# RWKV heads by column halves, and every engine's order from the library's timeline machine, in a two-layer hybrid decoder trunk

## The chip, the cores and the metric

One NeuronCore of a Trainium2 chip runs the whole program in one launch. The metric is the device time of that launch in microseconds (us), as the median of several runs. Engines are named as in the profile: PE (TensorE, the matmul engine, with its weight loads shown apart as PEld), DVE (VectorE), ACT (ScalarE), POOL (GpSimd), SP (SyncE, which issues DMAs).

## The reference

The input `x` is 1024 tokens by 1024 features, in float32. Each of two layers normalises it, projects it, runs four mixers side by side, gates and concatenates their outputs, projects back and adds a gated embedding:

```python
for i in range(DEPTH):
    proj = rms_norm(x, g_pre[i]) @ w_in[i]
    ...
    y_a = nsa_attention(...)
    y_b = spatial_gating(...)
    y_c = conv_module(...)
    y_d = rwkv7_time_mix(token_shift(rw, rwkv_mu[i]), ...)
    mix = jnp.concatenate([y_a * silu(z_a), y_b * silu(z_b), y_c * silu(z_c), y_d * silu(z_d)], axis=-1)
    x = x + rms_norm(mix @ w_out[i], g_post[i])
    x = x + sigmoid(x @ ple_gate[i]) * (p[i] @ ple_proj[i])
```

The change touches the fourth mixer, a recurrence over the tokens with one 64x64 state for each of four heads:

```python
def step(state, inp):
    r_t, w_t, k_t, v_t, kk_t, a_t = inp
    sa = einsum('bhvk,bhk->bhv', state, -kk_t)
    state = state * w_t + outer(sa, kk_t * a_t) + outer(v_t, k_t)
    return state, einsum('bhvk,bhk->bhv', state, r_t)
```

The attention mixer, whose matmuls share PE with it, has for every 128 queries and each of four heads three softmax branches: over compressed keys, over all earlier keys and over a window of 512.

## The kernel before

**Tiling.** Features lie on the 128 partitions and tokens along the free axis. The program goes through layer 0 and layer 1, each in two halves of 512 tokens. One letter of the strings `ORDER` (L32) stands for one stage of a half: `H` normalises, `F` prepares RWKV, `R` and `r` are its solve and its steps, `A` is one tile of 128 queries of attention, `a` to `d` and `N`, `G` are projections, `O`, `x`, `g` the output side. An `A` may belong to the half before. `run` emits the stages in this order, and `tail` (L1130) the end of the last half.

**Dense matmuls.** `mm3` (L161) forms one product of float32 precision from three matmuls of a high and a low part (L163, L164, L165). These are the dense matmuls below: mostly 128x512 each, the operands `aT` (activations) and `wh`, `wl` (weights, which `split_w`, L149, loads and splits), the results in PSUM banks named `mm`.

**PSUM.** Eight banks of 128x512: `mm` and `s` two each, `rp`, `pt`, `pv` and `c1` (shown as `c`) one each.

**Attention.** `branch` (L975) computes the scores into `s` (L994, L995), adds tables and takes maxima (L1014, L1018, L1022 on DVE), takes the exponential on ACT (L1024) and scales on DVE (L1029); its result is `r`. `attn_tile` then takes up to two blocks of keys for two heads at once: four transposes into the bank `pt` (L957), a copy to a high part on ACT (L960), a subtraction for the low part on DVE (L961), and two matmuls for each block into `pv` (L966, L967).

**RWKV.** A half has 8 chunks of 64 tokens. `rwkv_ab` (L509) forms for one chunk the matrices of the four heads (`a_block`, L430; L438 on PE into `rp` or `c1`; L516 on DVE masks them into `AT`, shown as `at`; L519, L521 transpose `BK` into `bkt`). `rwkv_solve` (L444) gets inverses of triangular 16 and 32 blocks of all heads and chunks with a loop on DVE: 15 rounds of L478 and L480, 16 of L500 and L502, through DRAM scratch `Nd` and `Xd`. `rwkv_tri` (L524) joins the blocks of a chunk to 64 (L533 on PE, L535 on DVE, L539 on PE, L541 on DVE, result `XF`). `rwkv_step` (L558) then moves the state `S` (two alternating tiles `SB`) over one chunk: four matmuls of one head each into `p1` (L578) and two of the state (L582), an ACT copy to `Wt` (L585, the tile `q`), four matmuls with `XF` (L589), copies into `uv` (the tile `l`) on DVE and ACT (L591, L592), four matmuls into `p3` (L602), four updates of the state on DVE (L611), four matmuls for the chunk's output (L616) and an ACT copy into `ytok` (L618, the tile `yt`). There are 32 steps: 8 for each of four halves.

In all of these matmuls of one head the four heads follow as 0, 1, 2, 3. Head `h` has pair `j = h // 2` and `e = h % 2`. L578, L533 and L616 write the same 64 output partitions for all four heads (L578 128 for head 0); L589 writes partitions 64 j to 64 j + 63; L602 those of e. Output partitions are the columns of PE's array, so L589 is in one column half for heads 0 and 1 and in the other for 2 and 3. The partitions of the operands are its row halves.

**What sets the order.** The kernel text gives a program order; the library's `TileContext` schedules every engine's instructions from it, with the program order as priority (weights are raised by `high_priority`, L151), and inserts the semaphore waits. Each engine then runs its list strictly in order: an instruction that waits holds up all behind it on the same engine. [...]

## Time and profile before

| | |
|---|---|
| median of 3 runs | 1925.44 us (1922.86 to 1941.99) |
| the profiled execution's own time | 1919.29 us |
| its span in the trace | 1917.6 us |
| mean granted PE clock in it | 0.954 |
| busy share: PE, DVE, ACT, POOL | 90%, 72%, 42%, 32% |

Shares are busy time over the span, of one execution. A row of a timeline gives start and duration in us, the engine, the line of the kernel, the operation, output and input tiles, their shapes, and how many equal instructions in a row it stands for. Matmuls overlap, and the end of one is modelled; the start of the next is the better measure of how long one took. DMA, at a third of its engines' time over the span, is not followed further here.

### The profile page before, as it was taken

The page shows a single profiled execution, that of the slowest core. Times are in us where ns is not written, and L with a number is a line of the kernel's source. Part 1 is how long each engine was busy: PE and PEld are TensorE (multiplying, and loading weights), DVE is VectorE, ACT ScalarE, POOL GpSimd, SP SyncE. Part 2 cuts the span into 40 slices and gives each one's busy share as a digit, 9 for nine tenths or more (in the row PEclk, how much of TensorE's full clock was granted, in tenths as well). Part 3 has the DMA queues.
Part 4 walks back from the last instruction along what each step waited for, and adds up shares of the span by engine and source line. Part 5 has one row for each costly group of instructions (what it writes and reads, how often), then busy time and mean ns, then how long its engine had stood idle before and what let it go on. Part 6 is the DMA issues. An engine that isn't in the chain of part 4 may idle for free. (4 is left out here: it accounts for less than half of the span.)

```text
span 1917.6 us, 27663 instructions
## 1 busy us (share of the span) xinstructions
PE 1725.0 (90%) x9444; PEld 1296.7 (68%) x9444; DVE 1383.7 (72%) x3361; ACT 813.6 (42%) x1805; POOL 612.2 (32%) x487
## 2 busy tenths in 40 slices
PE   5797998899799999899888999989988989989998
PEld 4565776566577667666666767766666767766777
DVE  4449787887888865977578881869778789476554
ACT  4332234544223455655232343545432445545543
POOL 2223343122342333322233346322232232422253
PEclk8898999999899999999998999999998999979999
DMA  6435233123432231532253233542253223223444
GB/s 208 90 87 107 71 97 84 45 57 64 114 81 78 67 99 63 169 106 55 60 123 78 69 115 117 166 121 56 62 113 79 53 57 115 66 72 109 139 139 152
DMA packets 326148, 182.23 MB, mean 95 GB/s; under 512 B 88300, under 2 KB 299248, under 8 KB 326008
## 3 DMA queue, kind: packets, MB, share of 16 engines
q1 hardware_dynamic: 326008, 180.47, 34.7%
q8 instruction: 74, 1.21, 0.3%
q14 instruction: 66, 0.54, 0.1%
HBM read 149.98 MB, written 30.44 MB: 94 GB/s over the span
## 5 line engine op out<-in xcount | busy, mean ns | idle before, releaser
L158 POOL TENSOR_TENSOR wl<-ws,wh 128x512 fp32r<-128x512 f32 (+2 forms) x388 | 521.6, 1346 | 1160.7 <-ACT wh L157 1021.0
L163 PE MATMUL mm<-aT,wh 128*128 128x512 f32 (+1 forms) x1304 | 538.2, 416 | 16.6 <-ACT t L667 7.4
L164 PE MATMUL mm<-aT,wh 128*128 128x512 f32 (+1 forms) x1304 | 536.3, 411 | 8.3 <-DVE aT L252 8.0
L165 PE MATMUL mm<-aT,wl 128*128 128x512 f32 (+1 forms) x1304 | 535.4, 411 | 0.4 <-POOL wl L158 0.4
L157 ACT CAST wh<-ws 128x512 fp32r<-128x512 f32 (+2 forms) x388 | 236.9, 611 | 454.3 <-PE mm L164 229.4
L163 PEld LDWEIGHTS mm<-aT,wh 128*128 128x128 f32 (+1 forms) x1304 | 251.0, 193 | 71.0 <-ACT t L667 7.9
L164 PEld LDWEIGHTS mm<-aT,wh 128*128 128x128 f32 (+1 forms) x1304 | 252.1, 193 | 60.5 <-DVE aT L252 15.2
L165 PEld LDWEIGHTS mm<-aT,wl 128*128 128x128 f32 (+1 forms) x1304 | 251.6, 193 | 48.2 <-issue 2.6
L683 DVE SCALAR_TENSOR_TENSOR cv<-cv,cw,cv 128x512 f32<-128x512 f32 x240 | 213.4, 905 | 3.2
L961 DVE TENSOR_TENSOR pt<-pt,pt 128x512 fp32r<-128x512 f32 (+1 forms) x152 | 93.7, 617 | 122.2 <-ACT pt L960 120.9
L1024 ACT ACTIVATE r<-s,sma 128x512 f32<-128x512 f32 (+3 forms) x192 | 106.2, 555 | 111.2 <-DVE sma L1022 76.3
L960 ACT CAST pt<-pt 128x512 fp32r<-128x512 f32 (+1 forms) x152 | 80.3, 528 | 112.7 <-PE pt L957 112.3
L957 PE MATMUL pt<-cst,r 128*128 128x128 f32 x528 | 98.4, 282 | 21.9 <-DVE r L1029 16.9
L957 PEld LDWEIGHTS pt<-cst,r 128*128 128x128 f32 x528 | 64.2, 143 | 50.8 <-DVE r L1029 26.3
L967 PE MATMUL pv<-pt,vs 128*128 128x256 f32 x264 | 79.0, 317 | 11.8 <-DVE pt L961 10.2
L966 PE MATMUL pv<-pt,vs 128*128 128x256 f32 x264 | 84.7, 321 | 2.4 <-ACT pt L960 2.1
L994 PE MATMUL s<-kv,qs 128*128 128x512 f32 (+2 forms) x192 | 75.6, 394 | 4.9 <-ACT r L1024 4.7
L1029 DVE TENSOR_SCALAR r<-r,sma 128x640 f32<-128x640 f32 (+7 forms) x128 | 76.1, 595 | 0.8
L967 PEld LDWEIGHTS pv<-pt,vs 128*128 128x128 f32 x264 | 50.6, 192 | 35.1 <-DVE pt L961 28.3
L966 PEld LDWEIGHTS pv<-pt,vs 128*128 128x128 f32 x264 | 50.6, 192 | 32.3 <-ACT pt L960 26.7
L995 PE MATMUL s<-kv,qs 128*128 128x512 f32 (+2 forms) x192 | 65.7, 345 | 0.0
L994 PEld LDWEIGHTS s<-kv,qs 128*128 128x128 f32 x192 | 37.1, 193 | 34.5 <-ACT r L1024 27.2
(333 smaller groups left out, 2904.1 us busy)
## 6 DMA issues: line engine op xcount, KB each, us to landing
ws<-in_w_in_dram SPq DMA_DIRECT2D x232, 256.0 KB, 2.9
ws<-in_ple_gate_dram SPq DMA_DIRECT2D x64, 256.0 KB, 2.8
ws<-in_w_out_dram SPq DMA_DIRECT2D x60, 256.0 KB, 2.8
ped<-ot SPq DMA_DIRECT2D x32, 256.0 KB, 3.4
ld<-in_nsa_w_dram SPq DMA_DIRECT2D x32, 256.0 KB, 3.5
ld<-ped SPq DMA_DIRECT2D x32, 256.0 KB, 3.5
mixd<-y SPq DMA_DIRECT2D x30, 256.0 KB, 2.0
ld<-mixd SPq DMA_DIRECT2D x30, 256.0 KB, 3.0
```

Source lines behind the costliest of these rows:

```text
L157: nc.scalar.copy(hi[:, :cols], st[:, :cols])
L158: nc.gpsimd.tensor_sub(lo[:, :cols], st[:, :cols], hi[:, :cols].bitcast(F32))
L163: nc.tensor.matmul(out, lh, rh, start=first, stop=False, skip_group_check=shared)
L164: nc.tensor.matmul(out, lh, rl, start=False, stop=False, skip_group_check=shared)
L165: nc.tensor.matmul(out, ll, rh, start=False, stop=last, skip_group_check=shared)
L683: nc.vector.scalar_tensor_tensor(ac, xg[j][:, k:k + TH], cw[:, j * 31 + k:j * 31 + k + 1], ac, op0=OP.mult, op1=OP.add)
L957: nc.tensor.transpose(pt[:, o:o + 128], P[e][:, (b + x - b0) * 128:(b + x - b0) * 128 + 128], self.ident)
L961: nc.vector.tensor_sub(Tl[:, :n], pt[:, :n], Th[:, :n].bitcast(F32))
L966: nc.tensor.matmul(acc, vs, Th[:, x * 256:x * 256 + 256], start=False, stop=False)
L967: nc.tensor.matmul(acc, vs, Tl[:, x * 256:x * 256 + 256], start=False, stop=last)
L994: nc.tensor.matmul(p[:, :n], w.QS[hd][:, qs], w.KH[br, hh][:, c0 * 128:c1 * 128], start=True, stop=False)
L1024: nc.scalar.activation(P[:, o:o + wd], p[:, c:c + wd], AF.Exp, bias=ng[:, 0:1], accum_out=den[:, x:x + 1])
```

## The change

There are two edits.

**Heads by column halves.** The heads are taken in the order 0, 2, 1, 3, and the operands are laid out so that pair `j` writes the output partitions 64 j to 64 j + 63. For pair 1 the two halves of `AR`, and with them those of `AT`, change places, and the mask `C_MA` is 64 columns wider, so that pair 1 reads it 64 columns on. `XF` and `Wt` become 128 partitions by 128 columns, each pair in its own half. One operation on all four heads therefore becomes one on each pair in several places: L535 and L541 on DVE become two each, the copy to `Wt` becomes one on ACT and one on DVE (2 x 128 columns in place of 256), the copy into `ytok` two on ACT, and the transfer of the first four chunks of a half to `Nd` two on SP. `a_block` becomes `a_blocks`, which takes two banks and alternates its matmuls between them.

**The order.** `TileContext` is called with `schedule_with_timeline_sim=True`: the lists of all engines are computed anew, with the library's model of when each instruction would run. The program order and its priorities are unchanged.

```diff
-    def a_block(self, q, c, e, full):
+    def a_blocks(self, q, c, full):
-        pA = self.ps("c1" if self.solving and self.nb % 2 else "rp")
+        pA = [self.ps("rp"), self.ps("c1" if self.solving else "s")]
         for j in range(2):
-            bk, ar = self.BK[j][q][es, c], self.AR[j][q][es, c]
+            for e in range(2):
+                es = slice(64 * e, 64 * e + 64)
+                bk, ar = self.BK[j][q][es, c], self.AR[j][q][es, c]
...
     def rwkv_solve(self):
             self.rwkv_ab(c)
-            nc.sync.dma_start(Nd[:, c * 256:c * 256 + 256].rearrange("p (h t) -> p h t", h=4),
-                              self.AT[c][0:64, :, :, 0:64].rearrange("p a b c -> p (a b) c"))
+            for j in range(2):
+                nc.sync.dma_start(Nd[:, c * 256 + j * 128:c * 256 + j * 128 + 128].rearrange("p (h t) -> p h t", h=2),
+                                  self.AT[c][0:64, j, :, 64 * j:64 * j + 64])
...
     def rwkv_tri(self, c):
-        for h in range(4):
-            nc.tensor.matmul(pT[0:64, hs[h]], N[h], XY[0:64, hs[h]], start=True, stop=True)
+        for h in (0, 2, 1, 3):
+            j, e = divmod(h, 2)
+            nc.tensor.matmul(pT[pair[j], hs[h]], self.AT[c][0:64, j, e, pair[j]], XY[0:64, hs[h]], start=True, stop=True)
-        nc.vector.tensor_mul(T1, pT[0:64, :256].rearrange("p (a b) -> p a b", a=4),
-                             self.c[0:64, C_ML:C_ML + 64].unsqueeze(1).to_broadcast([64, 4, 64]))
+        for j in range(2):
+            nc.vector.tensor_mul(T1[:, 2 * j:2 * j + 2], pT[pair[j], cols[j]].rearrange("p (a b) -> p a b", a=2),
+                                 self.c[pair[j], C_ML:C_ML + 64].unsqueeze(1).to_broadcast([64, 2, 64]))
-        for h in range(4):
-            nc.tensor.matmul(pX[64:128, hs[h]], T1[:, h], XY[64:128, hs[h]], start=True, stop=True)
-        XF = self.t([64, 4, 64], "xf", bufs=4)
-        nc.vector.tensor_add(fl(XF), XY[64:128], pX[64:128, :256])
+        for h in (0, 2, 1, 3):
+            nc.tensor.matmul(pX[pair[h // 2], hs[h]], T1[:, h], XY[64:128, hs[h]], start=True, stop=True)
+        XF = self.t([128, 2, 64], "xf", bufs=4)
+        for j in range(2):
+            nc.vector.tensor_add(XF[pair[j]].rearrange("p a b -> p (a b)"), XY[64:128, cols[j]], pX[pair[j], cols[j]])
...
     def rwkv_step(self, c):
-        for h in range(4):
+        for h in (0, 2, 1, 3):
             hs = slice(h * 64, h * 64 + 64)
-            m = 64 if h else 128
-            nc.tensor.matmul(p1[:m, hs], AT[64:128, h // 2, h % 2, :m], uv[64:128, hs], start=(h == 0), stop=False,
+            j, e = divmod(h, 2)
+            nc.tensor.matmul(p1[pair[j], hs], AT[64:128, j, e, pair[j]], uv[64:128, hs], start=(e == 0), stop=False,
                              skip_group_check=True)
...
-        Wt = self.t([128, 256], "q1", bufs=1)[:64]
-        nc.scalar.copy(Wt, p1[0:64])
-            nc.tensor.matmul(p2[es, h % 2 * 64:h % 2 * 64 + 64], XF[:, h], Wt[:, hs], start=False, stop=True,
+        Wt = self.t([128, 256], "q1", bufs=1)[:, :128]
+        nc.scalar.copy(Wt[0:64], p1[0:64, 0:128])
+        nc.vector.tensor_copy(Wt[64:128], p1[64:128, 128:256])
+            nc.tensor.matmul(p2[pair[j], e * 64:e * 64 + 64], XF[pair[j], e], Wt[pair[j], e * 64:e * 64 + 64],
...
-            nc.tensor.matmul(p1[64:128, hs], AT[:n, h // 2, h % 2, 64:128], uv[:n, hs], start=False, stop=True,
+            nc.tensor.matmul(p1[pair[1 - j], hs], AT[:, j, e, pair[1 - j]], uv[:, hs], start=False, stop=True,
-        nc.scalar.copy(ytok[64 * (c % 2):64 * (c % 2) + 64], p1[64:128])
+        for j in range(2):
+            nc.scalar.copy(ytok[pair[c % 2], j * 128:j * 128 + 128], p1[pair[1 - j], j * 128:j * 128 + 128])
...
-    with _tile.TileContext(nc) as tc:
+    with _tile.TileContext(nc, schedule_with_timeline_sim=True) as tc:
```

Lines of the functions behind `rwkv_solve` stand some numbers lower in the changed file: L578 is L582 there, L582 is L586, L589 is L593, L616 is L620, L957 is L962, L966 and L967 are L971 and L972.

Three places on PE show what the order does. The first is one RWKV step in the first half of layer 0. In before, PE's list has (`c_374` is the bank of the step, `mm` that of a projection, `x4` means four alike in a row):

```order
L578 MATMUL c_374_1685<-l_372_1678,at_1521 128x64
L578 MATMUL c_374_1685<-l_372_1678,at_1521 64x64 x3
L582 MATMUL c_374_1685<-SB_79,ab_447 128x128
L582 MATMUL c_374_1685<-SB_79,ab_629 128x128
L165 MATMUL mm_2337<-aT_306,wl_2359 128x512
L163 MATMUL mm_2337<-aT_311,wh_2358 128x512
L164 MATMUL mm_2337<-aT_312,wh_2358 128x512
L589 MATMUL c_374_1685<-q_375_1692,xf_1549 64x64 x4
L165 MATMUL mm_2337<-aT_311,wl_2359 128x512
L163 MATMUL mm_2337<-aT_316,wh_2358 128x512
```

The same step in the changed kernel:

```order
L582 MATMUL c_374_1717<-l_372_1710,at_1543 64x64 x4
L586 MATMUL c_374_1717<-SB_79,ab_447 128x128
L586 MATMUL c_374_1717<-SB_79,ab_629 128x128
L962 MATMUL pt_2909<-cst,r_638_2895 128x128
L962 MATMUL pt_2909<-cst,r_632_2881 128x128
L962 MATMUL pt_2909<-cst,r_638_2895 128x128
L593 MATMUL c_374_1717<-q_375_1724,xf_1572 64x64 x4
L999 MATMUL s_2973<-kv_1041,qs_1217 128x256
L1000 MATMUL s_2973<-kv_1042,qs_1217 128x256
L971 MATMUL pv_2879<-pt_2914,vs_1134 128x256
L606 MATMUL c_374_1717<-l_372_1710,bkt_1555 64x64 x4
```

Between the step's matmuls before has dense ones, and the changed kernel transposes, scores and products of attention, which an ACT and a DVE instruction must precede. The dense matmuls of this half have moved ahead of the steps: from one dense matmul of `mm_2551` to the next, of `mm_3792`, PE's list holds 379 others. I call this stretch A.

The second place is the loop of an attention tile late in the program. Before (one round of `pt_16374` and `pv_16317`, the dense matmuls of `mm_17531` among them):

```order
L957 MATMUL pt_16374<-cst,r_3924_16319 128x128
L957 MATMUL pt_16374<-cst,r_3931_16340 128x128
L957 MATMUL pt_16374<-cst,r_3924_16319 128x128
L957 MATMUL pt_16374<-cst,r_3931_16340 128x128
L163 MATMUL mm_17531<-aT_17154,wh_17552 128x512
L164 MATMUL mm_17531<-aT_17155,wh_17552 128x512
L165 MATMUL mm_17531<-aT_17154,wl_17553 128x512
L163 MATMUL mm_17531<-aT_17162,wh_17552 128x512
L966 MATMUL pv_16317<-pt_16379,vs_9393 128x256
L164 MATMUL mm_17531<-aT_17163,wh_17552 128x512
L165 MATMUL mm_17531<-aT_17162,wl_17553 128x512
L967 MATMUL pv_16317<-pt_16380,vs_9393 128x256
```

The same loop in the changed kernel, from its last dense matmul on:

```order
L165 MATMUL mm_18067<-aT_17831,wl_18089 128x512
L971 MATMUL pv_15643<-pt_15690,vs_9469 128x256
L972 MATMUL pv_15643<-pt_15691,vs_9469 128x256
L971 MATMUL pv_15643<-pt_15690,vs_9469 128x256
L972 MATMUL pv_15643<-pt_15691,vs_9469 128x256
L962 MATMUL pt_15698<-cst,r_3704_15645 128x128
L962 MATMUL pt_15698<-cst,r_3711_15665 128x128
L962 MATMUL pt_15698<-cst,r_3704_15645 128x128
L962 MATMUL pt_15698<-cst,r_3711_15665 128x128
L971 MATMUL pv_15643<-pt_15703,vs_9469 128x256
L972 MATMUL pv_15643<-pt_15704,vs_9469 128x256
L971 MATMUL pv_15643<-pt_15703,vs_9469 128x256
```

The transposes are now followed at once by the products that need them, with nothing between. This goes on for 277 matmuls, up to the `dense_short` of `tail` (stretch C). Between the two, in layer 1's first half, lies a third such stretch of 308 matmuls, in which PE transposes `bkt`, forms `at` and does attention while DVE has the whole loop of `rwkv_solve` (stretch B). It begins so:

```order
L165 MATMUL mm_9422<-aT_8691,wl_9444 128x512
L519 MATMUL rp_9140<-cst,ab_8823 128x128
L519 MATMUL rp_9140<-cst,ab_9005 128x128
L438 MATMUL c_2185_9165<-ab_8821,ab_8823 128x128
L438 MATMUL c_2185_9165<-ab_9003,ab_9005 128x128
L971 MATMUL pv_6586<-pt_6635,vs_1134 128x256
L972 MATMUL pv_6586<-pt_6636,vs_1134 128x256
```

In before the longest run of PE matmuls without a dense one is 68.

## Rows read from the trace of the kernel before

**Rows 1.** The page's first part: busy us (share of the span) x instructions.

```profile
PE 1725.0 (90%) x9444; PEld 1296.7 (68%) x9444; DVE 1383.7 (72%) x3361; ACT 813.6 (42%) x1805; POOL 612.2 (32%) x487
```

**Rows 2.** Windows: stretch, us; busy us of each engine (instructions); PE clock, DMA share, GB/s.

```profile
core 0: us, PE busy (x) PEld busy (x) DVE busy (x) ACT busy (x) POOL busy (x), PEclk, DMA share, GB/s
...
150.00:200.00 50.00, 36.63 (x201) 27.24 (x201) 45.18 (x81) 10.41 (x22) 13.75 (x11) 0.80 0.46 105
...
1000.00:1050.00 50.00, 43.12 (x222) 31.63 (x221) 45.18 (x65) 10.32 (x20) 15.49 (x12) 0.90 0.35 89
1150.00:1200.00 50.00, 48.09 (x211) 38.60 (x210) 7.32 (x21) 20.61 (x41) 30.41 (x24) 0.97 0.38 115
100.00:1900.00 1800.00, 1645.93 (x9124) 1239.60 (x9123) 1334.15 (x3252) 771.40 (x1734) 584.22 (x459) 0.96 0.34 93
```

**Rows 3.** Timeline of PE, 194 to 202: start us, duration us, instruction, [idle before].

```profile
196.27 0.63 PE L165 MATMUL mm<-aT,wl 128*128 128x512 f32 x1
...
200.54 0.45 PE L163 MATMUL mm<-aT,wh 128*128 128x512 f32 x1
```

**Rows 4.** Timeline of all engines, 1752 to 1755: a round of the attention loop.

```profile
1752.35 0.60 PE L957 MATMUL pt<-cst,r 128*128 128x128 f32 x4
...
1752.99 0.59 ACT L960 CAST pt<-pt 128x512 fp32r<-128x512 f32 x1 [2.45 <-PE pt L957]
1753.02 0.39 PE L165 MATMUL mm<-aT,wl 128*128 128x512 f32 x1
...
1753.25 0.40 PE L163 MATMUL mm<-aT,wh 128*128 128x512 f32 x1
...
1753.61 0.69 DVE L961 TENSOR_TENSOR pt<-pt,pt 128x512 fp32r<-128x512 f32 x1 [1.11 <-ACT pt L960]
...
1754.81 0.60 PE L957 MATMUL pt<-cst,r 128*128 128x128 f32 x4
```

**Rows 5.** Groups by form, PE: the first dense line; its two others are alike.

```profile
L163 PE MATMUL mm<-aT,wh 128*128 128x512 f32 x1272 | 525.6, 415 | 14.1 <-ACT t L667 7.4 <-DVE y L648 5.4 <-ACT ot L1103 0.4
```

**Rows 6.** Timeline of all engines, 294 to 301: one RWKV step.

```profile
294.28 0.92 PE L578 MATMUL c<-l,at 64*128 64x64 f32 x8 [0.46 <-ACT yt L618]
...
295.93 0.37 ACT L585 COPY q<-c 64x256 f32<-64x256 f32 x1 [1.71 <-PE c L582]
...
296.35 0.46 PE L589 MATMUL c<-q,xf 64*64 64x64 f32 x8 [0.28 <-ACT q L585]
...
297.25 0.26 ACT L592 COPY l<-c 64x128 f32<-64x128 f32 x1 [0.42 <-DVE l L591]
...
298.34 1.17 DVE L611 SCALAR_TENSOR_TENSOR SB<-c,gc,q 64x64 f32<-64x64 f32 x4
...
299.99 0.82 PE L616 MATMUL c<-l,at 64*64 64x64 f32 x8
```

**Rows 7.** Timeline of PE, 1527 to 1531: the matmuls of `rwkv_tri`.

```profile
1527.76 0.67 PE L533 MATMUL rp<-x,at 64*64 64x64 f32 x8
```

**Rows 8.** Groups of DVE: line, instruction xcount | busy us, mean ns | idle before.

```profile
L961 DVE TENSOR_TENSOR pt<-pt,pt 128x512 fp32r<-128x512 f32 (+1 forms) x152 | 93.7, 617 | 122.2 <-ACT pt L960 120.9 <-PE s L995 0.5
L1029 DVE TENSOR_SCALAR r<-r,sma 128x640 f32<-128x640 f32 (+7 forms) x128 | 76.1, 595 | 0.8
L1014 DVE CUSTOM_DVE_ANT_0 s<-s,T 128x256 f32<-128x256 f32 (+1 forms) x144 | 53.8, 374 | 2.4 <-PE s L995 1.7
...
L1018 DVE TENSOR_REDUCE sma<-s 128x1 f32<-128x256 f32 (+3 forms) x120 | 51.5, 432 | 0.5
L500 DVE TENSOR_TENSOR q<-l,q 128x128 f32<-128x128 f32 (+7 forms) x64 | 45.1, 705 | 2.1
L611 DVE SCALAR_TENSOR_TENSOR SB<-c,gc,q 64x64 f32<-64x64 f32 x112 | 31.7, 283 | 7.3 <-PE c L602 5.0 <-ACT t L729 0.4 <-ACT t L1054 0.2
...
L535 DVE TENSOR_TENSOR q<-rp,cst 64x256 f32<-64x256 f32 x32 | 13.4, 418 | 13.6 <-PE rp L533 12.5 <-PE c L589 0.5
...
L591 DVE COPY l<-c 64x128 f32<-64x128 f32 x32 | 9.0, 282 | 13.4 <-PE c L589 9.4 <-ACT bkt L521 1.5 <-ACT t L732 1.1
```

**Rows 9.** Groups of ACT: the exponential of attention, same columns.

```profile
L1024 ACT ACTIVATE r<-s,sma 128x512 f32<-128x512 f32 (+3 forms) x192 | 106.2, 555 | 111.2 <-DVE sma L1022 76.3 <-PE pt L957 30.4 <-issue 2.5
```

More of the change, by code (lines that the diff above doesn't have):

```diff
@@ L95, in setup @@
             self.SB.append(x)
-        self.nsb = self.nq = self.nb = 0
+        self.nsb = self.nq = 0
         self.onec = self.const([128, 1], "onec")
@@ L525, in rwkv_tri @@
         nc = self.nc
-        fl = lambda x: x.rearrange("p a b -> p (a b)")
         hs = [slice(64 * h, 64 * h + 64) for h in range(4)]
-        N = [self.AT[c][0:64, h // 2, h % 2, 0:64] for h in range(4)]
+        pair = [slice(64 * j, 64 * j + 64) for j in range(2)]
+        cols = [slice(128 * j, 128 * j + 128) for j in range(2)]
         XY = self.t([128, 256], "x0", bufs=1)
@@ L1263, in _constants @@
     oh[:32] = (np.arange(32)[:, None] == bucket[None, :]).astype(float) - (np.arange(32)[:, None] == 31)
-    parts = [r == c, ma, low(32)[:, :64], p[:, None] % 32 == p[None, :32], far, hb, flag, hs]
+    parts = [r == c, ma, ma[:, :64], low(32)[:, :64] | low(32)[:, 64:], r % 32 == c[:, :32], far, hb, flag, hs]
     parts += [r + c == 127, oh]
```

39 lines of the change are left out of this document (18 added, 21 removed).

## The prediction, made before the result was known

> **What bounds the kernel now.** I read the page's first part, then windows of the span, then the timeline of the two loops that the change touches, and last the groups of DVE's instructions. TensorE (PE) is busy 90% of the span and VectorE (DVE) 72% [rows 1]: PE is the bound, with DVE close behind. The windows show how the two share the time [rows 2]. Where DVE has little to do (1150 to 1200, 7.32 us), PE is busy 48.09 of 50 us; where DVE is full (150 to 200 and 1000 to 1050, 45.18 us each) PE falls to 36.63 and 43.12 and its granted clock to 0.80 and 0.90. From 100 to 1900 PE is busy 1645.93 of 1800 us, 91.4%. In these windows DVE is never more than 90% busy, so what DVE bounds lasts about as long as the plain sum of its instructions, or longer.
>
> What keeps PE busy is the dense matmul. One of 512 columns follows the last every 0.23 us at full clock (1753.02 to 1753.25 [rows 4]) and every 0.43 at half: eleven from 196.27 to 200.54 [rows 3]. The attention loop cannot fill PE alone: four transposes into the single `pt` bank, an ACT copy of 0.59, a DVE subtraction of 0.69, the last `pv` matmul, and only then the next four transposes, which bank and order don't allow earlier. They start at 1752.35 and 1754.81: a round is 2.46 us, of which PE's attention work is some 0.9 by the starts there, and dense matmuls fill the rest [rows 4].
>
> For scale I need PE's pure issue time. 1272 matmuls of each of three dense lines [rows 5] at 0.23 us are 878 us; the other 5628 of the 9444 [rows 1] I put at 0.095, between a small one (eight records in 0.46 [rows 6]) and a dense one: 535 us. So some 1410 us, an estimate; the span is 1.36 us per us of it.
>
> **Part 1, heads by column halves.** In before a step runs eight records each of L578 in 0.92 us, of L616 in 0.82 and of L589 in 0.46 [rows 6]; L533 takes 0.67 [rows 7], and L539 has its shape. L589 alternates between column halves, the others stay in one. The change makes all of them alternate, and the new order keeps their four matmuls together. I price each at L589's 0.46: 32 steps x (0.46 + 0.36) + 32 chunks x 2 x 0.21 = 26 + 13 = 39 us less of PE. Bounds from the same rows: 0 (alternation of halves gives nothing) to about 50 (each at 0.4). L438 is written to alternate between row halves, but the order sets the two matmuls of one half side by side, as before: 0.
>
> L589 now changes row half and column half at once, while its heads write one bank. No row shows two row halves writing one bank; between 0.3 and 0.67 I keep 0.46, so 0 us. The Trainium skill, TensorEngine Tiling (Array Packing), Gotcha 1: PSUM Pressure, says that different row tiles cannot access the same bank simultaneously; by that L589 would be as slow as L533, 0.21 x 32 = 7 us more.
>
> Added: L535 (418 ns) and L541, of its shape, become two 64x128 halves each, which take 282 as in L591 [rows 8]: 32 x 2 x 0.14 = 9 us of DVE; 32 half copies of Wt on DVE, 9 us; on ACT the copy of 0.37 (L585) shrinks to 0.26 (the form of L592) and that of `ytok`, of L585's shape, becomes two of 0.26: 32 x (0.52 - 0.37 - 0.11) = 1 us [rows 6]. SP issues 16 more DMAs, halves of a transfer that DVE awaits only after four more a-blocks: 0 us, at worst 16 times the issue of one. The copy on DVE is a new wait: L589 now waits for DVE's queue, with PE's next matmuls behind it, and the next state update behind those. At worst half a subtraction of L961, 0.3 us, 32 times; I take 0, because the ACT half runs as long and dense matmuls cover it. In the stretches below there is no cover, and DVE's sum holds the copy.
>
> **Part 2, the order, decides.** The longest run of PE matmuls without a dense one is 68 in before; in after there are three of 379, 308 and 277. There nothing fills PE, so DVE or round trips set the length. I counted the DVE instructions that cannot start before PE's dense matmul ahead of the stretch and must end before the one behind it, took the means of [rows 8], and 0.28 us, the small forms' size (L611, L591), for the rest.
> A (end of layer 0's first half), 283: 28 L611 x 0.283, 17 L1014 x 0.374, 16 L1029 x 0.595, 32 halves of L535 and L541 x 0.282 are 33 us, 190 others 53: 86 us. PE's own work, by spacings as above: 49.
> B (layer 1's first half), 253: 16 L500 x 0.705, 20 L961 x 0.617, 19 L1018 x 0.432, 15 L1014, 11 L1029 are 44 us, 172 others 48: 92 us against 40 of PE.
> C (the last attention tiles), 195: 26 L961, 27 L1018, 22 L1014, 15 L1029 are 45 us, 105 others 29: 74 us against 36 of PE. Here round trips are longer: 26 x 2.46 = 64 us, and 7 times a softmax (0.37 + 0.43 on DVE, 0.56 on ACT, 0.60 on DVE [rows 8, 9]) stands open before the next transposes, 14 us: 78 us.
> Together 256 us for 125 us of PE work, which at the pace of before would take 125 x 1.36 = 170: +86 us. Bounds: -40, if DVE's instructions overlap by a seventh and nothing waits; +60, if chains add to DVE's sums (rival 3).
>
> The rest (1285 us of PE work) gains. 22 of the 32 steps and 20 of the 32 chunks stand there: 18 + 8 = 26 of the 39 us. With less attention and DVE work beside it PE should idle less: at the 96.2% of 1150 to 1200 it would save 1720 x (1 - 91.4/96.2) = 86 us; most of the RWKV and attention work still stands there, so I take a quarter, 22. And a stretch with PE half idle can leave a low clock, as 150 to 200 shows [rows 2]: eleven dense matmuls at 0.43 instead of 0.23, as from 196.27 [rows 3], cost 2.2 us, three times 7. The Trainium skill, TensorE: Matmul & The Clock Gate, Why this matters for your kernels, asks for no idle gaps between bursts, as the clock then falls back; the rows agree, and by it even more dense work behind each stretch could run at half.
>
> Sum on the profiled execution's own 1919.3 us: + 86 - 26 - 22 + 7 = 1964, so **1965 us**. That execution is 0.3% under the median of the runs, 1925.4; a measurement can tell about 1%, 19 us, from no change.
>
> **Rivals.** (1) Faster: the dense runs outside A, B and C, with no attention between them, go at the pace of 1150 to 1200. Gain 86 + 26, stretches at their low end +46: 1919 - 112 + 46 = 1853; at half that gain 1896. It decides from the point where the rest gains over 86 us. For it: 48.09 of 50 in [rows 2]; against it: 60% of the attention is still in the rest. (2) No change: stretches at the low end, the rest as priced, 1919 + 46 - 48 + 7 = 1924. (3) Worse: in A and B the RWKV steps and attention rounds wait for each other in PE's one order, so the chains add to DVE's sum: 5.2 us from L578 to the end of L611 [rows 6] x 8 = 42 in A, half in B: 2028. (4) The halves give nothing on PE: 1965 + 26 + 7 = 1998.
>
> **How the numbers follow.** My forecast 0.40, (3) 0.12, (4) 0.10, (2) 0.18, (1) 0.20. Slower by over 1% 0.62, within 1% 0.18, faster 0.20. The range 1880 to 2065 leaves out the far end of (1) and what lies beyond (3); the forecast's own is 1930 to 2005.
>
> **What would show it.** In after's profile: three stretches of 75 to 100 us with no dense matmul, DVE over 80% busy in A and B, PE far below its 91% and its clock low there; the last tiles' transposes 2.4 to 2.6 us apart; eight records of L578, L616, L533, L539 in about 0.46 us; PE above 92% elsewhere. It is wrong if the stretches last under 70 us each, or if PE outside them gains over 86 us.

## The result, and the profile after

The changed kernel takes 2188.87 us (median of 4 runs, 2184.67 to 2196.51). Against before, run beside it (1933.72), the ratio is 1.135 (95% interval 1.131 to 1.140). The direction was forecast, the size was not: 255 us slower instead of some 40. I read the profile after in the order of the prediction.

The page's first part, which answers to [rows 1]:

```profile
PE 1836.5 (84%) x9444; PEld 1403.5 (64%) x9444; DVE 1383.7 (63%) x3457; ACT 812.4 (37%) x1837; POOL 620.9 (28%) x487
```

The work is the same (9444 matmul records; DVE is busy for the same 1383.7 us, with 96 instructions more), but neither engine is near its limit any more. PE idles 354 us instead of 193, and its busy time grew by 111 us for the same records. The granted clock is lower: 0.839 on average, 0.954 before. The windows between the edges of the three bare stretches (last dense matmul to next) say where, as [rows 2] did for before:

```profile
core 0: us, PE busy (x) PEld busy (x) DVE busy (x) ACT busy (x) POOL busy (x), PEclk, DMA share, GB/s
0.00:276.40 276.40, 222.58 (x1053) 168.52 (x1054) 175.54 (x346) 91.58 (x172) 98.43 (x80) 0.91 0.46 115
276.40:407.10 130.70, 88.22 (x614) 66.03 (x612) 70.94 (x287) 37.97 (x118) 12.23 (x13) 0.59 0.10 29
407.10:974.30 567.20, 513.11 (x2708) 391.87 (x2709) 402.85 (x977) 233.22 (x516) 182.85 (x140) 0.90 0.32 88
974.30:1088.90 114.60, 84.25 (x402) 58.46 (x400) 74.41 (x260) 35.04 (x97) 2.51 (x3) 0.58 0.13 22
1088.90:1936.30 847.40, 742.47 (x4004) 582.91 (x4004) 548.75 (x1305) 331.47 (x742) 291.32 (x228) 0.90 0.34 96
1936.30:2069.90 133.60, 91.10 (x280) 61.73 (x278) 58.97 (x197) 38.73 (x112) 2.10 (x2) 0.52 0.01 4
2069.90:2190.40 120.50, 94.80 (x391) 73.97 (x391) 52.24 (x92) 44.36 (x83) 31.46 (x22) 0.83 0.32 98
```

The stretches A, B and C are there (the second, fourth and sixth row). They last 131, 115 and 134 us, 379 together, where I put 86, 92 and 78, or 256. DVE is busy 54%, 65% and 44% of them: it doesn't bound them, and its busy time (71, 74, 59 us) is under my counts. PE's clock is 0.52 to 0.59. The rest lasts 1811.5 us, where the forecast leaves 1708. So some 123 us of the miss lie in the stretches and 103 outside.

Two parts of C show what a stretch consists of. PE's transposes at its start, in the timeline of PE:

```profile
1936.95 0.60 PE L962 MATMUL pt<-cst,r 128*128 128x128 f32 x4
1938.22 0.38 PE L971 MATMUL pv<-pt,vs 128*128 128x256 f32 x1 [0.67 <-ACT pt L965]
...
1939.40 0.60 PE L962 MATMUL pt<-cst,r 128*128 128x128 f32 x4
1940.65 0.69 PE L999 MATMUL s<-kv,qs 128*128 128x384 f32 x1 [0.65 <-ACT r L1029]
...
1946.27 0.88 PE L962 MATMUL pt<-cst,r 128*128 128x128 f32 x3
...
1949.41 1.05 PE L962 MATMUL pt<-cst,r 128*128 128x128 f32 x4
```

The first round is 2.45 us, that of [rows 4] within 0.01; the clock is still up (four transposes in 0.60). Then it falls (four in 1.05), and a round takes 3.14. And between two branch pairs, in the timeline of all engines:

```profile
1991.92 0.63 PE L962 MATMUL pt<-cst,r 128*128 128x128 f32 x2
1992.42 0.69 ACT L1029 ACTIVATE r<-s,sma 128x512 f32<-128x512 f32 x1 [2.09 <-PE pt L962]
...
1995.12 0.68 DVE L1034 TENSOR_SCALAR r<-r,sma 128x896 f32<-128x896 f32 x1
...
1995.95 0.45 PE L962 MATMUL pt<-cst,r 128*128 128x128 f32 x1 [0.40 <-DVE r L1034]
...
1997.45 0.69 ACT L1029 ACTIVATE r<-s,sma 128x512 f32<-128x512 f32 x1 [1.50 <-DVE sma L1027]
...
1999.71 0.68 DVE L1034 TENSOR_SCALAR r<-r,sma 128x896 f32<-128x896 f32 x1
...
2000.45 0.90 PE L962 MATMUL pt<-cst,r 128*128 128x128 f32 x3 [0.60 <-DVE r L1034]
```

The first head's exponential waits for the last transposes of the pair before, the second head's for DVE's maxima behind it, and both chains run one after the other: 8.5 us from the last transposes to the next full set. I had priced 2.46 + 2. In the whole of C that happens seven times, five of 6.6 to 8.5 us and two of 16, where the tile changes: 69 us instead of the 31 in my sum. These 38 us are most of C's 56 us over the forecast; the 17 rounds at the low clock (3.23 us each on average, for 2.46) make some 13 more, an estimate.

### The profile page after: what moved, and what is told of

It reads as the page before. It is cut to its first block, busy times and chain, and to the rows that moved or that the text cites. A ratio compares the mean times of both kernels' runs of the same rounds, so it can differ in the third digit from the quotient of the medians.

```text
span 2190.4 us, 27860 instructions
## 1 busy us (share of the span) xinstructions
PE 1836.5 (84%) x9444; PEld 1403.5 (64%) x9444; DVE 1383.7 (63%) x3457; ACT 812.4 (37%) x1837; POOL 620.9 (28%) x487
## 5 line engine op out<-in xcount | busy, mean ns | idle before, releaser
L158 POOL TENSOR_TENSOR wl<-ws,wh 128x512 fp32r<-128x512 f32 (+2 forms) x388 | 533.6, 1378 | 1147.1 <-ACT wh L157 1114.6
L163 PE MATMUL mm<-aT,wh 128*128 128x512 f32 (+1 forms) x1304 | 547.7, 421 | 38.6 <-DVE t L738 13.8
L164 PE MATMUL mm<-aT,wh 128*128 128x512 f32 (+1 forms) x1304 | 538.4, 413 | 5.0 <-DVE aT L252 5.0
L163 PEld LDWEIGHTS mm<-aT,wh 128*128 128x128 f32 (+1 forms) x1304 | 258.3, 198 | 108.7 <-DVE t L738 16.3
L164 PEld LDWEIGHTS mm<-aT,wh 128*128 128x128 f32 (+1 forms) x1304 | 257.6, 198 | 62.1 <-DVE aT L252 6.3
L688 DVE SCALAR_TENSOR_TENSOR cv<-cv,cw,cv 128x512 f32<-128x512 f32 x240 | 225.8, 961 | 1.7
L966 DVE TENSOR_TENSOR pt<-pt,pt 128x512 fp32r<-128x512 f32 (+1 forms) x152 | 93.8, 617 | 125.9 <-ACT pt L965 125.2
L962 PE MATMUL pt<-cst,r 128*128 128x128 f32 x528 | 120.8, 337 | 23.5 <-DVE r L1034 19.2
L971 PE MATMUL pv<-pt,vs 128*128 128x256 f32 x264 | 100.6, 383 | 33.6 <-ACT pt L965 33.4
L999 PE MATMUL s<-kv,qs 128*128 128x512 f32 (+2 forms) x192 | 93.7, 489 | 26.5 <-ACT r L1029 25.4
L972 PE MATMUL pv<-pt,vs 128*128 128x256 f32 x264 | 97.9, 382 | 18.2 <-DVE pt L966 12.9
L962 PEld LDWEIGHTS pt<-cst,r 128*128 128x128 f32 x528 | 79.3, 170 | 43.0 <-DVE r L1034 24.4
L971 PEld LDWEIGHTS pv<-pt,vs 128*128 128x128 f32 x264 | 63.8, 242 | 58.6 <-ACT pt L965 52.4
L602 POOL TENSOR_TENSOR q<-SB,gc 128x256 f32<-128x256 f32 x28 | 18.9, 675 | 253.1 <-DVE SB L613 124.7
L972 PEld LDWEIGHTS pv<-pt,vs 128*128 128x128 f32 x264 | 63.6, 241 | 37.3 <-DVE pt L966 31.3
L1000 PE MATMUL s<-kv,qs 128*128 128x512 f32 (+2 forms) x192 | 78.7, 414 | 0.0
```

The source lines that it names most:

```text
L158: nc.gpsimd.tensor_sub(lo[:, :cols], st[:, :cols], hi[:, :cols].bitcast(F32))
L163: nc.tensor.matmul(out, lh, rh, start=first, stop=False, skip_group_check=shared)
L164: nc.tensor.matmul(out, lh, rl, start=False, stop=False, skip_group_check=shared)
L688: nc.vector.scalar_tensor_tensor(ac, xg[j][:, k:k + TH], cw[:, j * 31 + k:j * 31 + k + 1], ac, op0=OP.mult, op1=OP.add)
L962: nc.tensor.transpose(pt[:, o:o + 128], P[e][:, (b + x - b0) * 128:(b + x - b0) * 128 + 128], self.ident)
L966: nc.vector.tensor_sub(Tl[:, :n], pt[:, :n], Th[:, :n].bitcast(F32))
```

## The experiments

**The halves and the order apart.** Two kernels, each with one of the two edits.

```diff
-    with _tile.TileContext(nc, schedule_with_timeline_sim=True) as tc:
+    with _tile.TileContext(nc) as tc:
```

> The changed kernel with the library's default order (the schedule flag left out), so the column halves alone. Theory (the order empties stretches of dense matmuls, the granted clock falls to half there, and everything on PE takes twice as long): no long bare stretch, clock about 0.95, 1890 to 1930 us, L582, L620, L534, L541 at about 0.46 us for eight records. Rival (the halves themselves cost: the DVE copy ahead of L593, one bank written by both row halves): over 2000 us, with L593 slower than 0.46 and PE waiting for DVE's copy. Rival of no effect of halves: within 5 us of before.

Measured: 1919.17 us, ratio 0.995 (0.993 to 0.998). The kernel before with only the flag:

> The kernel before with only the schedule flag. Theory (order and clock): bare stretches of PE (its list has runs of 504, 206 and 181 matmuls with no dense one), clock 0.82 to 0.87, 2150 to 2240 us, as slow as the changed kernel or slower by the 25 to 40 us that the halves save. Rival (the halves cost): 1920 to 1970 us.

Measured: 2106.81 us, ratio 1.093 (1.089 to 1.096). So the order does the harm, and the halves alone are a little faster than before. But the changed kernel is 82 us slower than the order alone, and that the second expectation had the wrong way round. The halves' own prices came out as forecast; from the timeline of PE and the groups of DVE with the halves alone:

```profile
267.39 0.45 PE L582 MATMUL c<-l,at 64*64 64x64 f32 x8
...
270.11 0.45 PE L593 MATMUL c<-q,xf 64*64 64x64 f32 x8 [0.82 <-DVE q L590]
```

```profile
L537 DVE TENSOR_TENSOR q<-rp,cst 64x128 f32<-64x128 f32 x64 | 18.5, 289 | 11.6 <-PE rp L534 10.6
L544 DVE TENSOR_TENSOR xf<-x,rp 64x128 f32<-64x128 f32 x64 | 18.3, 286 | 6.2 <-PE rp L541 4.6
...
L590 DVE COPY q<-c 64x128 f32<-64x128 f32 x32 | 9.4, 293 | 4.1 <-ACT q L589 3.5
```

**The clock in the bare stretches.** In the next four kernels extra matmuls of 256 columns go into unused columns of the `pv` bank, so that PE has more to do and nothing of the result changes. In the first two, behind the products of each round of the last two tiles, ten or three:

```diff
                         nc.tensor.matmul(acc, vs, Tl[:, x * 256:x * 256 + 256], start=False, stop=last)
+                    if w.l and w.h and t > 1:
+                        for _ in range(10):
+                            nc.tensor.matmul(pv[:, 256:512], vs, Th[:, :256], start=False, stop=False, skip_group_check=True)
```

> The changed kernel with ten more matmuls of 256 columns in each attention round of the last two tiles (28 rounds, 280 matmuls into unused columns of the pv bank, nothing of the result changes). PE's order elsewhere is that of the changed kernel. Theory (clock): PE is kept busy in stretch C, the granted clock stays near 1.0 there, rounds go back to 2.5 us, and C falls from 134 us to 80 to 105; the whole 25 to 50 us less than the changed kernel, although it does 280 matmuls more (34 us at full clock). Rival (the chain of ACT and DVE sets the stretch whatever the clock): C stays at 134 us or grows by up to 34, and the clock in it may rise with no gain.

> As the run with ten, with three more matmuls in each of the 28 rounds (84). Clock theory: too few to keep the clock up all the time; C between the ten-matmul run and 134 us, or, if the clock stays at half, about 134 + 84 x 0.22 x 1/2 = 143 us at most. Rival (chains): C 134 us, the three hidden behind ACT and DVE at either clock.

Measured: 2202.08 and 2201.34 us (1.142 and 1.141, each within 0.005). With ten the clock in C rose to 0.77 and C grew to 151 us; with three it stayed at 0.55 and C took 145. The first is the rival's outcome, the second near the 143 of a clock that stays at half. Neither settles the matter, as the placement was bad: in the timeline the ten stand between a round's last product and the next transposes, in series, 1.2 us each time even at full clock (25 us in the 21 rounds that lie in C, which grew by 17). So they were moved into the gaps, five behind the transposes, three behind the first product, twelve between pairs:

```diff
+                    if late and (b > b0 or br):
+                        for _ in range(5 if b > b0 else 12):
+                            nc.tensor.matmul(pv[:, 256:512], vs, Tl[:, :256], start=False, stop=False, skip_group_check=True)
                     Th, Tl = self.t([128, TH], "pt", dt=F32R), self.t([128, TH], "pt", dt=F32R)
...
                         nc.tensor.matmul(acc, vs, Th[:, x * 256:x * 256 + 256], start=False, stop=False)
+                        if late and x == 0:
+                            for _ in range(3):
```

> The changed kernel with 232 more matmuls of 256 columns in the last two attention tiles, this time where PE waits anyway: five behind the transposes of a round (ACT copies), three behind the first pv matmul (DVE subtracts), twelve between two branch pairs. Nothing of the result changes, and the order elsewhere stays. Theory clock-as-a-part (the chain of softmax and rounds sets stretch C, and the half clock lengthens its PE links): rounds of four transposes fall from 3.2 to about 2.5 us, C from 134 to 105 to 120 us, the whole 10 to 30 us under the changed kernel. Rival A (the clock alone makes C long): C falls to 80 to 95 us, the whole 40 to 55 under. Rival B (the clock costs nothing): C 134 us or more.

> The same fillers in the last two tiles of layer 0's second half, which lie in stretch B beside the solve loop on DVE. Theory: B falls from 115 to 100 to 108 us, less than C, since DVE's own sum is 74 us there. Rival A (clock alone): to 80. Rival B: 115 or more.

Measured: 2175.56 us (1.129, 1.124 to 1.134) with the fillers in C, 2196.82 (1.139, 1.135 to 1.143) in B. The window of C with them, and one round in PE's timeline:

```profile
1942.30:2069.00 126.70, 91.73 (x453) 71.96 (x451) 58.34 (x197) 38.81 (x111) 2.12 (x2) 0.76 0.02 5
```

```profile
2060.83 0.60 PE L962 MATMUL pt<-cst,r 128*128 128x128 f32 x4
2061.18 0.83 PE L967 MATMUL pv<-pt,vs 128*128 128x256 f32 x5
...
2063.35 0.38 PE L962 MATMUL pt<-cst,r 128*128 128x128 f32 x2
```

Where the clock is up, the round is 2.5 us again, and C is 7 us shorter, although PE does 174 matmuls more in it (of the 232); the whole is 13 us shorter (medians; the intervals just overlap). C missed its 105 to 120 us, with a clock of only 0.76. B went from 115 to 110 us at a clock of 0.80, but it takes 110 to 115 in the runs that leave it alone too, so no gain is shown there, nor in the whole. That the clock alone makes the stretches long doesn't fit: half of what was lost came back (0.52 to 0.76), and 7 of C's 56 us. That the stretch is a chain whose links the half clock lengthens fits; what a full clock would be worth in C wasn't measured.

**Cover moved back.** The next kernels each move one or two pieces of the new order, or change a bank. The second head's scores of a pair go to the banks `c1` and `rp`:

```diff
-            p = self.ps("s")
+            p = self.ps(("c1", "rp")[hh] if w.l and w.h and i > 5 and hd % 2 else "s")
```

> The changed kernel, where in the last two tiles the second head of each branch pair puts its scores into the banks c1 and rp, free by then, in place of the two s banks. Theory (between two branch pairs some 8 us pass because the second head's scores wait until the first head's exponential has read the two s banks): 8 pairs, 2 to 4 us less each, C 134 to 105 to 118 us, the whole 15 to 30 us less. Rival (the wait is for the two buffers r of the exponentials, or for the clock): C 130 to 136 us.

Measured: 2204.17 us (1.143, 1.138 to 1.148), and the two tiles still have 3.1 to 3.3 us for nearly every round and 6.3 to 8.5 for a change of pair, so the two `s` banks were not what these wait for. It is no clean test of the whole, as the order came out differently: C became two bare stretches of 90 and 88 us behind each other. The scores are there early, but DVE's list takes the second head's maxima only behind the first head's sums. Next, the tail's first output projection waits for tile 1 through a dependency:

```diff
+            x = self.ld(blk(mixd, k))
+            nc.vector.scalar_tensor_tensor(x[:, 0:128], za[1][:, 128:256], 0.0, x[:, 0:128], op0=OP.mult, op1=OP.add)
+            return self.split_cm(x)
```

> The changed kernel, where the dense matmuls of the tail's first output projection (144 of 512 columns, 33 us at full clock) cannot start before the attention tile before the last two has ended: a dependency that adds zero times a value of that tile, six DVE operations of about 0.3 us. So part of the cover returns to stretch C. Theory (the order took the cover away): C's 134 us now hold the 33 us of dense work at little cost (at most 145 us in all from the end of tile 1 to the dense matmuls of the tail's short part), and the place where they stood before C loses up to 33: the whole 10 to 33 us less. Rival (the place before C had idle time for them too, so that nothing is saved): within 8 us of the changed kernel.

Measured: 2191.70 us (1.135, 1.129 to 1.141): the rival. C's bare part shrank to 90 us, and a bare stretch of 48 us opened in the tile ahead. The convolution taps wait for the first step (weights copied through zero times the state):

```diff
+            if c == 0:
+                self.cwd = self.t([128, 62], "cwd", bufs=2)
+                nc.vector.scalar_tensor_tensor(self.cwd, SN[:, 0, 0:62], 0.0, self.cw[:, :62], op0=OP.mult, op1=OP.add)
```

> The changed kernel, where the 60 convolution taps of a half cannot start before the first RWKV step of that half has written its state: their weights are copied through an operation that adds zero times that state (one DVE operation a half). DVE's list then has the whole solve loop, and the first steps, ahead of the taps; in the changed kernel the taps stand ahead of or between the solve's operations and ahead of the steps in three of the four halves. Theory (the new order runs filler work, taps on DVE and dense matmuls on PE, as a block ahead of the chains, so that the chains start late and then run bare): steps of the first, second and fourth half start 20 to 60 us sooner than at 303, 638 and 1689 us, DVE is busier in stretch A, and the whole takes 2040 to 2140 us. Rival (PE's order, in which all dense matmuls of a half stand ahead of the steps, alone sets the start of the steps): within 15 us of the changed kernel.

and, the other way round, the halves in the default order with the taps as a block ahead of the solve:

```diff
-ORDER = ("iXeHFBRNrGabscdnAAATCy",
+ORDER = ("iXeHFBGTRNrabscdnAAACy",
...
```

> The opposite, with the column halves and the library's default order: the stage of the convolution's taps (and the projection it needs) stands ahead of the RWKV solve in the program order of each half, so that DVE's list has the 60 taps as a block ahead of the solve; PE's longest run without a dense matmul is 132. Theory: each half's chain starts later by the 45 to 55 us of the block, of which dense matmuls cover a part: 1960 to 2080 us, with step 0 of the halves 20 to 50 us later than at 220, 554, 1042 and 1474. Rival (filler ahead of the chains costs nothing as long as dense matmuls stand beside the chains): 1900 to 1940 us.

Measured: 2190.93 us (1.135, 1.130 to 1.140) and 2040.47 (1.057, 1.051 to 1.063). The second is what the theory said: work that is only filler costs over 100 us (2040 against 1919) if it stands ahead of a chain, in the default order too; step 0 of the four halves came 60, 94, 130 and 168 us later than with the halves alone, more than the 20 to 50 expected, as the delays add up. The first is the rival: step 0 came 21, 14, 7 and 41 us sooner in the four halves, and step 7 at the same time (373, 778, 1288 and 1793 us, against 377, 780, 1275 and 1793), since the taps now lie among the steps. Last of this group, the gate projections wait for the first step, alone and together with the taps:

```diff
-            nc.scalar.copy(hi[:, :cols], st[:, :cols])
+            if self.hold:
+                nc.scalar.activation(hi[:, :cols], st[:, :cols], AF.Identity, bias=self.zdep[:, 0:1])
```

> The changed kernel, where the weights of the gate projections (stages a to d, 192 dense matmuls each half, 44 us at full clock) cannot be split before the first RWKV step of that half has written its state (the copy to the high part becomes an Identity with a bias of zero times that state). PE's list then has 336, 499 and 453 dense matmuls between the first and the last step of the first, second and fourth half, in place of 0, 336 and 180; its longest runs without a dense one are 296, 213 and 193. Theory (dense matmuls run ahead of the chains and are missing beside them): step 0 of the first half at 220 to 260 us in place of 303, PE busy over 80% with a clock over 0.8 beside those steps, and the whole 60 to 160 us less than the changed kernel. Rival (cover that is moved leaves a hole where it stood, as with the tail's matmuls, and the chains are as long as before): within 20 us of the changed kernel.

> Both holds together: gate projections and convolution taps wait for the first step. Theory: with dense matmuls beside the chains the taps beside them no longer matter for PE, and the solve is free of them, so that this is faster than the hold of the projections alone by 10 to 60 us. Rival (the taps beside the steps lengthen DVE's part of the chain as much as they shortened the solve, as in the run with the taps alone held): within 10 us of the hold of the projections.

Measured: 2212.73 us (1.146, 1.141 to 1.151) and 2202.19 (1.141, 1.136 to 1.146): against the theory, although step 0 of the first half came at 264 and 238 us instead of 303. The windows of the first show the hole that the held matmuls left, beside the solve of the first and the fourth half:

```profile
200.00:250.00 50.00, 2.41 (x30) 1.97 (x32) 34.88 (x84) 1.04 (x2) 0.00 (x0) 0.50 0.10 13
1600.00:1650.00 50.00, 2.08 (x24) 1.57 (x24) 36.57 (x81) 1.06 (x2) 1.86 (x1) 0.50 0.10 13
```

**The bank `s`.** What had made the changed kernel slower than the order alone? PE's list gave the clue: its longest runs are those of the order alone as soon as the a-blocks in the steps keep out of `s`.

```diff
-        pA = [self.ps("rp"), self.ps("c1" if self.solving else "s")]
+        if self.solving:
+            pA = [self.ps("rp"), self.ps("c1")]
+        for e in range(2):
+            p = pA[e] if self.solving else self.ps("rp")
...
```

> The changed kernel, where a_blocks outside the solve takes the bank rp for both of its results one after the other, as a_block did, and leaves the two s banks to attention. PE's list then has the long runs of the order alone (503, 201, 181 matmuls, against 504, 206, 181 there and 379, 308, 277 in the changed kernel). Theory (what makes the changed kernel slower than the order alone is the s bank that the a-blocks take from attention's scores, which turns the library's order over): 2060 to 2110 us, the order alone's 2107 less what the halves save. Rival (the halves cost in this order by their own instructions): 2170 us or more.

> The kernel before with the schedule flag and with a_blocks of the changed kernel (banks rp and s side by side, matmuls alternating), but without anything else of the column halves. PE's list has the long runs of the changed kernel (379, 338, 277). Theory (the s bank): 2180 to 2230 us. Rival (the other parts of the halves make the difference): 2090 to 2130 us, as the order alone.

> The column halves with the library's default order and a_blocks in one bank as in the first of these runs. Theory: in the default order the bank matters little, as the halves alone with it took 0.995 of before: 0.985 to 1.0 of before. If the s bank costs attention there too, it is faster than the halves with it by over 0.5%.

Measured: 2079.71 us, 2231.30 us and 1921.98 us. Ratios to before (95% intervals within 0.005):

| | default order | new order |
|---|---|---|
| no halves, a-blocks in `rp` | 1 (before) | 1.093 |
| no halves, a-blocks in `rp` and `s` | not run | 1.159 |
| halves, a-blocks in `rp` | 0.996 | 1.080 |
| halves, a-blocks in `rp` and `s` | 0.995 | 1.135 (the change) |

In the new order the `s` bank costs 2231 - 2107 = 124 us without the halves and 2189 - 2080 = 109 with them; the halves save 2107 - 2080 = 27 and 2231 - 2189 = 42. (The runs without the bank also take the four matmuls of `a_blocks` in another order; that was not separated from the bank.) In the default order neither the bank nor the rest is worth more than some 10 us. The windows of the scores' line alone (L999 in the changed kernel, L1001 in the one without the bank; columns: PE busy of that line and its count, clock, DMA share, GB/s) show how. The changed kernel:

```profile
150.00:250.00 100.00, 0.00 (x0) 0.90 0.40 95
250.00:300.00 50.00, 0.00 (x0) 0.75 0.35 79
...
1550.00:1650.00 100.00, 0.00 (x0) 0.82 0.40 90
1650.00:1750.00 100.00, 0.77 (x1) 0.86 0.30 90
```

Without the bank:

```profile
150.00:250.00 100.00, 2.92 (x9) 0.90 0.39 93
250.00:300.00 50.00, 1.98 (x4) 0.76 0.37 79
...
1550.00:1650.00 100.00, 4.35 (x12) 0.86 0.36 88
1650.00:1750.00 100.00, 7.54 (x16) 0.74 0.19 55
```

Without the bank, attention has 13 scores by 300 us, while the solve still runs, and 28 from 1550 to 1750. With it there are none and one (of this line; L1000 has as many). Who holds the banks is in the timelines of the changed kernel, PE's (a-blocks into `s`, and the first score) and DVE's (the mask that reads such an a-block and frees its bank):

```profile
90.76 0.71 PE L438 MATMUL s<-ab,ab 64*128 64x128 f32 x4
...
126.81 0.71 PE L438 MATMUL s<-ab,ab 64*128 64x128 f32 x4
...
335.17 0.56 PE L999 MATMUL s<-kv,qs 128*128 128x256 f32 x1
```

```profile
308.57 0.42 DVE L516 TENSOR_TENSOR at<-rp,cst 128x256 f32<-128x256 f32 x1 [0.80 <-PE c L620]
308.92 0.41 DVE L516 TENSOR_TENSOR at<-s,cst 128x256 f32<-128x256 f32 x1
318.36 0.42 DVE L516 TENSOR_TENSOR at<-s,cst 128x256 f32<-128x256 f32 x1
```

The inputs of the a-blocks are ready early, so the new order writes those of the fifth and the sixth chunk at 91 and 127 us, one into each of the two `s` banks. Their masks write the tiles `at`, of which there are four, and the first four chunks hold these until the steps have read them (step 0 is at 302.6, and the first mask waits for its L620), so the masks run only at 309 and 318. For some 200 us attention has no bank for a score, although PE would have had time for one: without the bank 32 of the 384 score matmuls run ahead of step 0. In the default order the a-blocks take the banks too (153 us to a first mask at 227 in the kernel with the halves alone) and hold up the first scores (271 us, against 166 with the a-blocks in `rp`), but only four matmuls stand so early there, and the ratio is the same with the bank and without it. In the changed kernel's other halves the banks are held from 548 to 657 and 670 us, from 1127 to 1164 and 1196, and from 1543 to 1702 and 1719; in the fourth the first score (1734.69) follows a mask of `s` (1731.94).

The 109 us come out behind the last step. In the profiled runs the last half's step 7 is at 1792.5 us with the bank and at 1796.8 without, and from there to the end (the same windows of L999 and L1001):

```profile
1792.50:2190.40 397.90, 31.07 (x54) 0.75 0.24 74
1796.80:2088.70 291.90, 12.77 (x26) 0.82 0.33 101
```

The attention that found no bank is done there, with the same dense matmuls left in both (648) and twice the score matmuls (108 for 52): 398 us instead of 292.

**What the order alone costs.** With the bank out of the way, the taps were held once more:

> The changed kernel without the s bank in a_blocks (2080 us), where the convolution taps also wait for the first step's state, as in the run that held them before. In the run without the s bank the taps stand between the solve's operations in three of the four halves: the first 15 rounds take 59, 59 and 61 us there against 13 where none stand between. Theory (with the s bank gone attention can run while the chain waits, and what is left of the order's cost is largely the taps that stretch the solve): the solves take 13 to 20 us each, the steps start 20 to 45 us sooner in the first, second and fourth half, and the whole takes 1980 to 2050 us. Rival (as with the s bank, what the solve gains the steps lose again beside the taps): 2060 to 2095 us.

Measured: 2089.89 us (1.084, 1.079 to 1.089): the rival again. Then the matmuls of the later stages were put back behind the RWKV front, by the same bias, now zero times the masked fourth a-block; alone, and with the taps held too:

```diff
                 for step in ORDER[2 * l + h]:
+                    self.hold = step in "NGabcd"
...
+        nc.vector.tensor_scalar(self.zdep[:, 0:1], self.AT[3][:, 0, 0, 0:1], 0.0, None, op0=OP.mult)
```

> The changed kernel without the s bank in a_blocks (2080 us), where the weights of the stages N, G and a to d of a half cannot be split before the masks of the fourth a-block are written (the copy to the high part becomes an Identity with a bias of zero times that result). PE's list then has 216, 936, 2088 and 3240 dense matmuls ahead of the solve's last a-blocks, as in before (223, 955, 2097, 3252), in place of 355, 1076, 2160 and 3379. Theory (the new order lets the dense matmuls of later stages run among those of the RWKV front, so that each half's solve starts 20 to 50 us late): the solve starts within 110 us of the end of the half's norm, as in before, in place of 156, 151, 122 and 142 us, and the whole takes 1960 to 2040 us. Rival (cover that is moved leaves a hole, as in every run that held something so far): 2060 to 2100 us.

> The same with the convolution taps held until the first step's state as well. Theory: the solve is free of taps too, 10 to 30 us less than the run that holds the front alone. Rival (as twice before): within 12 us of it.

Measured: 2077.99 us (1.075, 1.071 to 1.079) and 2068.73 (1.071, 1.067 to 1.075), against 2079.71 without a hold: the rival in both. The first solve starts at 157 us instead of 191, but only 11 us of all this reach the end. In the last kernel the solve is as short as in before, and then the first half's steps take 109 us (from the second chunk's state update at 278 to the last at 387), where they take 68 in before (231 and 299): attention now runs among them (36 score matmuls from step 0 to step 7, for 4). So no single piece of the order explains its 140 to 180 us; what is left is not settled.

## Why the prediction was wrong, point by point

**What bounds before** held: the rows were read rightly, and the round of attention reappears (2.45 us for 2.46) where the clock is up.

**Part 1** was right in its prices. Each eight records of L582, L620, L534 and L541 take 0.45 us, where I took 0.46; L593 stays at 0.45, although its matmuls write one bank from both row halves (each row half into its own 64 partitions; both in the same ones is not shown here). The 7 us that the Trainium skill's TensorEngine Tiling (Array Packing), Gotcha 1: PSUM Pressure, would have added are not there, so the measurement decides against it here. DVE's halves take 289, 286 and 293 ns, for 282. The 39 us that I took off PE agree with the 27 and 42 us that the halves save in the new order, though there the lists differ too. In the default order only some 10 of them reach the end: PE's busy time fell from 1725 to 1717 us, and its clock from 0.954 to 0.937.

**The step that failed first** is "L438 is written to alternate between row halves ...: 0". I priced the matmuls of `a_blocks` and not its second bank. In the steps that bank is `s`; filled early and read late, it keeps attention out, and it costs 109 us (124 without the halves). No other single change within the new order gave back as much, and no rival had it. The 109 us are not in addition to the 123 and 103 above: they are part of the same time, seen by what undoes it. Without the bank the kernel would still lie 115 us above the forecast (2080), so the next two steps failed as well.

**Part 2** had the right place, and all three stretches were found; the price was wrong in two terms. "DVE or round trips set the length" took PE's work there at full clock and DVE's as a sum without gaps. Shown is a chain: DVE busy 44 to 65%, rounds of 3.1 to 3.3 us at a clock of 0.52 to 0.59. In C "7 times a softmax ... 14 us" was the worst term: 69 us for 31 (with a round each). The clock, which I charged only behind a stretch (7 us), works inside it, some 13 us in C's rounds by the estimate above; giving PE filler brought 7 us back in C. The Trainium skill's TensorE: Matmul & The Clock Gate, Why this matters for your kernels, asks for no idle gaps between bursts; here the clock fell after gaps of 0.34 to 0.67 us (1938 to 1941), shorter than those that the page names.

**"The rest ... gains"**, 48 us in the sum (26 and 22), is the other wrong step. The rest lost instead: 1811.5 us, with PE 87% busy (1573 of 1811.5) and a clock of 0.83 to 0.91: 103 us over the forecast's 1708. I took fewer chains in the rest for less idle time. But in before dense matmuls stood beside the chains in every half, and the new order moved them. Windows of L163 alone (every third dense matmul) show it. Before, to the first half's step 0 and on to its step 7:

```profile
0.00:219.40 219.40, 72.43 (x167) 0.89 0.48 118
219.40:294.00 74.60, 20.57 (x57) 1.00 0.30 81
```

The changed kernel, the same:

```profile
0.00:302.60 302.60, 105.47 (x256) 0.88 0.44 110
302.60:377.40 74.80, 0.00 (x0) 0.55 0.07 20
```

All 256 are done before step 0, which comes 84 us later (302.6 against 218.6), and none is left beside the steps. The seven steps take 75 us each time, so in this half the lost time lies ahead of them. In the others it does not. From step 0 to step 7 (first matmul into `p1` of each), with the dense matmuls in between:

| half | 1 | 2 | 3 | 4 |
|---|---|---|---|---|
| before: us, dense matmuls | 76, 173 | 79, 156 | 74, 160 | 77, 155 |
| changed: us, dense matmuls | 75, 0 | 141, 336 | 212, 474 | 103, 180 |

The third half's steps in windows of L163, before and changed:

```profile
1045.80:1120.20 74.40, 18.62 (x54) 1.00 0.26 70
1063.00:1275.40 212.40, 64.33 (x158) 0.83 0.26 70
```

There the new order puts the filler not ahead of the chain but between its steps: one of them takes 51 us with 187 dense matmuls in it. All 32 steps together last 226 us longer than before, and the stretches ahead of and between the halves' steps are no shorter for it (1261 us, for 1252). Why they are not stays open. Of the rivals (3), chains that add to DVE's sums, was nearest in kind, and far too small.

## What to carry to other kernels

The order from the library's timeline spent the filler ahead of the chain in one half and put two or three times as much of it between the chain's steps in two others; a hand-made program order no longer protected the chains. Before such a switch, compare the list of before and after for long runs without filler, but price such a run by the chain through all engines and not by the busiest one's sum. When an edit borrows a bank or buffer from another stage, ask how long it is held there: a bank that is filled early and read late blocks its owner in between. Here that cost 109 us, and only in the order that overlaps the two stages; it came out at the end of the program, where the work that had waited was left over. Moving filler back by a dependency leaves a hole where it stood; seven such runs brought half a per cent at most.

The halves alone, in the default order, are the best version that ran: 0.995 of before (0.993 to 0.998), not to be told from the same with the a-blocks in `rp` (0.996).

## What the runs showed of the hardware that was not expected

Eight 64x64 records that change row half and column half with every matmul, all into one bank, took 0.45 us, as fast as those that change the column half only; in one column half they had taken 0.82 to 0.92 [rows 6]. And the granted clock recovers inside a chain-bound stretch if PE is given matmuls in its gaps (0.52 to 0.76 in C with 174 of them in it), but the stretch shortens by only 5%, from 133.6 to 126.7 us.
